# Attention of a hybrid encoder layer: the first product of the next pair but one begun within a pair's last two blocks, and a third gate of the sample made there

## The chip, the cores and the metric

The kernel runs on one core of one Trainium2 chip. The metric is the device time of one execution in microseconds. The median of the three runs of the kernel before is 2042.07 us (2040.25 to 2045.98).

The engines go by the names of the profile: PE is TensorE's matmul side and PEld its loading of weights, DVE is VectorE, ACT is ScalarE, POOL is GpSimd, SP is SyncE, which issues most DMAs. Each engine works through its own queue in order.

## The reference, cut to what matters

One encoder layer is applied to two groups of tokens, a prompt (1 x 1024 tokens) and a sample (1 x 512 tokens), each with 16 learned meta tokens in front. D_MODEL is 1024, there are 8 attention heads of 64, and the grid of tokens is 64 wide, so the prompt has 16 rows and the sample 8.

```
def encoder_layer(x, w_in, rel_bias, meta_bias, w_branch_na, w_branch_fn, w_out, g_mix, g_mlp, w_up, w_down):
    h = rmsnorm(x, g_mix)
    z = h @ w_in
    q, k, v, u, gate_na, gate_fn = jnp.split(z, ...)
    y_na = neighbourhood_attention(q, k, v, rel_bias, meta_bias) @ w_branch_na
    y_fn = fourier_mix(u) @ w_branch_fn
    mixed = sigmoid(gate_na) * y_na + sigmoid(gate_fn) * y_fn
    x = x + mixed @ w_out
    a = relu(rmsnorm(x, g_mlp) @ w_up)
    return x + (a * a) @ w_down
```

In neighbourhood_attention each grid token attends to 8 rows x 16 columns around it and to the 16 meta tokens. All is float32.

## The kernel before, in words

**Order of the whole.** The sample goes first, then the prompt. For each of the two, `run` (L328) reads and normalizes the tokens into hT (the normalized input, transposed, tokens along the free axis), projects the values, runs `attention` (L470), then `gates` (L720: the two gates of 1024 channels as 16 products with a sigmoid, 8 slices of 128 channels each), the merge of the attention branch, the Fourier branch, the output projection and the MLP.

**Precision.** A float32 product is made of three matmuls on operands that are split into a high and a low part: high x high, high x low, low x high. For a weight, ACT writes the high part (L151, or L154 with a scale) and another engine the low part (L152 on POOL or, where `lo_engine` says so, on DVE; L155 on DVE). `weights` (L141) loads a raw weight tile over SP's queue (L145) and splits it. The raw, high and low tiles have two buffers each, so a weight can be split only when the product before the last has ended.

**Attention.** Heads are handled in four pairs (`pr` 0 to 3). `project(pr)` (L493) is a generator that makes k and q of a pair: k in chunks of positions (two of 264 for the sample; 352, 344 and 344 for the prompt), q in chunks of 512 (one for the sample, two for the prompt). Each chunk is a `product` (L483) of eight steps of three matmuls (L487 to L489), and the generator yields after each step; after the eighth it evicts the chunk (L521 to L531 for k, L543 with L132 and L133 for q). At its very start it fetches and splits the weights of k and q (L495), takes the four tiles for q and k (L496, L497; four buffers per kind, that is two pairs' worth) and has POOL write the zero columns of k (L502).

`units(pr)` (L567) yields the pair's blocks: 8 for the sample and 16 for the prompt. A block (`unit`, L575) is itself a generator of three stages:

- scores: two matmuls (L594, L595), then bias and maximum on DVE (L599), the exponential on ACT (L601), reciprocal and scaling on DVE (L602, L603);
- transposes of the scores on PE into a PSUM tile `ps_t` of which there are two (L607), split by ACT (L132) and DVE (L133) into `pt`;
- the products with the values (L627), and after four blocks the eviction through `ot` (L632, one buffer) and `os` (L633), stored by L636.

`step` (L662) runs the first stage of a block together with the second stage of the block two before it and the third stage of the block four (sample) or three (prompt) before it. After each of the three it calls `between`.

**What is fed in between.** While a pair's blocks run, `feed` takes steps from a chain `nxt` (L672): the projections of the next pair, then steps of `early_gates` (L638), which makes some of the first gate's slices ahead of time: 24 matmuls a slice in the sample, evicted through `ot` (L646) and stored to DRAM (L647); `gates` loads them back (L728) and only applies the sigmoid (L735). `quota` (L657) says how many products of 512 positions of the gates are fed in each pair: none, none, none and 2 for the sample, 4, 2, 2 and 4 for the prompt. The number of steps, with four more that are empty, is spread evenly over the first slots of the pair; a block has three slots, and except in the last pair the two last blocks are left out of the count:

```
slots = 3 * (nu + lags[-1] if pr == 3 else nu - 2)
step(x, lambda s: feed(min(steps, (3 * u + s + 1) * steps // slots)))
```

With 28 steps (24 and the four empty ones) over 18 slots in the sample's pairs 0 to 2, the last real step falls into the sixth of eight blocks, and the two last blocks get none. Pair 3 has 16 real steps over 36 slots, the last 12 of which belong to the stages that run out.

**Gates.** `gates` runs over eight slices and makes, for each, first the attention gate (skipped where it was made early) and then the Fourier gate. Beside its products it runs generators from a list `beside` (L386 to L393), each with the count of the first product and the end: `fold_u` beside products 0 to 7 and `fold` (the folding of positions) beside products 6 to 13. There are 14 products in the sample.

**Order within a queue.** The framework plans each engine's queue from the program: an instruction comes as early as its inputs and its engine allow by the plan, and the earlier one in the program goes first where several could. `pinned` and `behind` (L110, L114) hold an instruction behind earlier ones. On the chip the queues then run in the planned order.

## Time and profile before

| what | value |
|---|---|
| median of three runs | 2042.07 us |
| lowest and highest run | 2040.25, 2045.98 us |
| profiled execution, its own time | 2044.82 us |
| span of its instructions | 2043.0 us |
| mean granted PE clock | 0.986 |
| sample's attention, first scores to last value product | 70.44 to about 162.0 us |
| prompt's attention, first scores to last value product | 824.27 to about 1049 us |

The profile's page gives, for each engine, the busy time, its share of the span and the number of instructions. The view of busy time by windows gives the same for stretches of time, with the clock that PE was granted: 1.00 is full speed. The view of waits says for which engine and line an engine's instructions waited. The timeline lists instructions in order of time, with the idle time of the engine ahead of one and what ended it in square brackets. The chain is the sequence of work that ended last, followed back from the end.

### The profile page before, as it was taken

The page shows a single profiled execution, that of the slowest core. Times are in us where ns is not written, and L with a number is a line of the kernel's source. Part 1 is how long each engine was busy: PE and PEld are TensorE (multiplying, and loading weights), DVE is VectorE, ACT ScalarE, POOL GpSimd, SP SyncE. Part 2 cuts the span into 40 slices and gives each one's busy share as a digit, 9 for nine tenths or more (in the row PEclk, how much of TensorE's full clock was granted, in tenths as well). Part 3 has the DMA queues.
Part 4 walks back from the last instruction along what each step waited for, and adds up shares of the span by engine and source line. Part 5 has one row for each costly group of instructions (what it writes and reads, how often), then busy time and mean ns, then how long its engine had stood idle before and what let it go on. Part 6 is the DMA issues. An engine that isn't in the chain of part 4 may idle for free.

```text
span 2043.0 us, 26403 instructions
## 1 busy us (share of the span) xinstructions
PE 1958.7 (96%) x9611; PEld 1626.4 (80%) x9611; DVE 1135.8 (56%) x1913; ACT 755.5 (37%) x1322; POOL 955.7 (47%) x744
## 2 busy tenths in 40 slices
PE   6989979999999999999999999999999999999997
PEld 4877867788888878888888888787788878888886
DVE  6572535667665553566663235567777677342246
ACT  3564413333333231455562313124333333533342
POOL 3224525366677641132243225203787785644442
PEclk9999989999999999999999999999999999999999
DMA  6655872345544445454555444322445444976663
GB/s 203 168 140 187 233 222 86 106 132 179 160 135 144 155 160 204 113 137 127 138 184 176 127 123 133 111 69 76 165 145 198 146 171 168 314 236 204 194 192 124
DMA packets 275363, 325.96 MB, mean 160 GB/s; under 512 B 42840, under 2 KB 197208, under 8 KB 274680
## 3 DMA queue, kind: packets, MB, share of 16 engines
q1 hardware_dynamic: 261504, 303.40, 46.7%
q0 software_dynamic: 13728, 20.88, 4.5%
q8 instruction: 75, 1.23, 0.3%
q14 instruction: 56, 0.46, 0.1%
HBM read 235.41 MB, written 91.37 MB: 160 GB/s over the span
## 4 chain that ended last, share of the span: by engine, by line
PE 82%; DVE 7%; DMA 3%; issue 2%; ACT 2%; POOL 2%; SPq 0%; ACTq 0%; DVEq 0%; POOLq 0%
PE ps_mm L128 22%; PE ps_o L128 20%; PE ps_s L128 18%; PE ps_t L128 7%; PE ps_mm L487 3%; PE ps_mm L488 3%; PE ps_mm L489 3%; PE ps_o L627 2%; PE ps_t L607 1%; DVE hn L873 1%; DVE gate L878 1%; POOL w_lo L152 1%; PE ps_s L594 1%; DVE gate L872 1%; DMA w_raw<-in_w_in 1%
## 5 line engine op out<-in xcount | busy, mean ns | idle before, releaser
L152 POOL TENSOR_TENSOR w_lo<-w_raw,w_hi 128x1024 fp32r<-128x1024 f32 x85 | 215.5, 2543 | 229.9 <-ACT w_hi L151 201.4
L151 ACT CAST w_hi<-w_raw 128x1024 fp32r<-128x1024 f32 x100 | 104.7, 1049 | 171.4 <-PE ps_s L128 48.9
L1056 DVE TENSOR_TENSOR relu<-relu 128x512 f32<-128x512 f32 (+1 forms) x34 | 66.7, 1960 | 108.2 <-ACT relu L1055 108.1
L487 PE MATMUL ps_mm<-hT,w_hi 128*128 128x512 f32 (+3 forms) x312 | 122.0, 391 | 0.0
L489 PE MATMUL ps_mm<-hT,w_lo 128*128 128x512 f32 (+3 forms) x312 | 113.0, 362 | 0.0
L488 PE MATMUL ps_mm<-hT,w_hi 128*128 128x512 f32 (+3 forms) x312 | 112.8, 361 | 0.0
L1293 POOL TENSOR_TENSOR x<-w_hi,x 128x512 fp32r<-128x512 f32 (+1 forms) x42 | 78.6, 1871 | 22.8 <-ACT x L1296 22.8
L601 ACT ACTIVATE sc<-sc,ast 128x288 f32<-128x288 f32 (+4 forms) x96 | 53.8, 561 | 83.8 <-DVE ast L599 83.0
L152 POOL TENSOR_TENSOR w_lo<-r,w_hi 128x1024 fp32r<-128x1024 f32 x15 | 35.9, 2395 | 95.3 <-ACT w_hi L151 95.3
L711 POOL MEMSET bm<- 64x96 f32 (+2 forms) x64 | 11.9, 185 | 143.2 <-DVE ast L599 98.8
L627 PEld LDWEIGHTS ps_o<-pt,vb 104*64 104x64 f32 (+6 forms) x576 | 62.5, 166 | 14.6 <-ACT pt L132 3.7
L627 PE MATMUL ps_o<-pt,vb 104*64 104x128 f32 (+6 forms) x576 | 65.5, 249 | 7.0 <-ACT pt L132 2.9
L152 POOL TENSOR_TENSOR w_lo<-w_hi 128x1024 fp32r<-128x1024 f32 x18 | 46.0, 2553 | 49.6 <-ACT w_hi L151 45.8
L128 PE MATMUL ps_t<-gate,x 128*128 128x512 f32 x264 | 65.5, 397 | 2.7 <-DVE r_lo L1404 2.7
L152 POOL TENSOR_TENSOR w_lo<-w_lo,w_hi 128x1024 fp32r<-128x1024 f32 x18 | 46.0, 2557 | 46.2 <-ACT w_hi L151 46.2
L489 PEld LDWEIGHTS ps_mm<-hT,w_lo 128*128 128x128 f32 x312 | 59.8, 192 | 8.0
L564 POOL TENSOR_TENSOR vb<-vr,vb 96x384 fp32r<-96x384 f32 (+4 forms) x48 | 48.4, 1023 | 37.8 <-ACT vb L563 37.7
L599 DVE CUSTOM_DVE_ANT_0 sc<-ps_s,bm 128x288 f32<-128x288 f32 (+4 forms) x96 | 46.3, 483 | 34.3 <-PE ps_s L595 18.2
L128 PE MATMUL ps_mm<-gate,x 128*128 128x512 f32 x256 | 64.2, 395 | 0.0
L487 PEld LDWEIGHTS ps_mm<-hT,w_hi 128*128 128x128 f32 x312 | 60.3, 193 | 2.3
L488 PEld LDWEIGHTS ps_mm<-hT,w_hi 128*128 128x128 f32 x312 | 60.4, 194 | 2.2
L128 PEld LDWEIGHTS ps_t<-gate,x 128*128 128x128 f32 x264 | 48.7, 188 | 16.1 <-DVE r_lo L1404 5.2
(670 smaller groups left out, 5885.3 us busy)
## 6 DMA issues: line engine op xcount, KB each, us to landing
w_raw<-in_w_in SPq DMA_DIRECT2D x56, 512.0 KB
w_raw<-in_w_up SPq DMA_DIRECT2D x34, 512.0 KB
wt<-hn SPq DMA_DIRECT2D x32, 512.0 KB
hidden_prompt<-h SPq DMA_DIRECT2D x32, 512.0 KB
w_hi<-hidden_prompt SPq DMA_DIRECT2D x20, 512.0 KB
w_raw<-hidden_prompt SPq DMA_DIRECT2D x18, 512.0 KB
w_lo<-hidden_prompt SPq DMA_DIRECT2D x18, 512.0 KB
w_raw<-in_w_out SPq DMA_DIRECT2D x16, 512.0 KB
```

Source lines behind the costliest of these rows:

```text
L128: self.nc.tensor.matmul(out, a, b, start=(i == 0 and not more), stop=(i == len(terms) - 1), skip_group_check=more)
L151: nc.scalar.copy(out=hi, in_=raw)
L152: (lo_engine or nc.gpsimd).tensor_tensor(out=lo, in0=raw, in1=hi.bitcast(F32), op=ALU.subtract)
L487: nc.tensor.matmul(ps, a[0], b[0], start=(kt == 0), stop=False)
L488: nc.tensor.matmul(ps, a[0], b[1], start=False, stop=False)
L489: nc.tensor.matmul(ps, a[1], b[0], start=False, stop=(kt == 7))
L564: nc.gpsimd.tensor_tensor(out=lo, in0=vs, in1=hi.bitcast(F32), op=ALU.subtract)
L599: nc.vector.tensor_tensor_reduce(out=sc[:, :W], in0=ps[:, :W], in1=bm[:, :W], scale=1.0, scalar=3e38, op0=ALU.add, op1=ALU.min, accum_out= ...
L601: nc.scalar.activation(out=sc[:, :W], in_=sc[:, :W], func=AF.Exp, bias=st[:, 0:1], scale=-1.0, accum_out=st[:, 1:2])
L627: nc.tensor.matmul(po[:m, j * 128:(j + 1) * 128], v, x, start=(i == 0), stop=(i == len(ops) - 1))
L1056: nc.vector.tensor_tensor(out=r, in0=r, in1=r, op=ALU.mult)
L1293: self.nc.gpsimd.tensor_tensor(out=to, in0=x, in1=y, op=op)
```

## The change

The change has three parts.

1. In `project`, the tiles for q and k and the zero columns on POOL are taken only after the eighth step of the first k product. The seven steps before need only the weights, hT and a PSUM bank.
2. The main loop of `attention` feeds steps in the two last blocks as well. The four empty steps go. All that is due in a pair is spread over the slots up to the two last blocks (in pair 3 over all slots); in the six slots of the two last blocks, seven steps of the *next but one* pair's projections are fed, 1, 1, 1, 1, 1 and 2. In pair 2, which has no next but one, the seven steps come from the early gates. The next pair then has seven steps fewer to do: 17 in the sample's pairs 1 and 2, 17 in its pair 3 (three gates, less seven); in the prompt 72, 49, 49 and 25.
3. The sample's last pair makes three early gates instead of two (`quota`), so that `gates` has 13 products instead of 14, and `fold` begins beside product 5 instead of 6.

The order of the products among themselves stays as it was.

```
-                          (fold, 6, 14)]
+                          (fold, 5, 13)]
...
         def project(pr):
             wk, wq = w0 if pr == 0 else self.qk_weights(pr)
-            qs = [p.tile([128, T], F32R, name="q", tag="q", bufs=4) for _ in range(2)]
-            ks = [p.tile([128, 2, nslot, 64], F32R, name="k", tag="k", bufs=4) for _ in range(2)]
-            state[pr] = (qs, ks)
             halves = slice(0, 64), slice(64, 128)
-            for k in ks:
-                for s in (0, nslot - 1):
-                    nc.gpsimd.tensor_copy(k[:, :, s, 16:64].rearrange("p i (g c) -> p i g c", g=2)[:, :, :, 0:8],
-                                          self.zero[:, None, None, 0:8].to_broadcast([128, 2, 2, 8]))
...
             for ci, (c0, cn) in enumerate(kch):
                 ps = self.psum("mm" if pr else None)
                 yield from product(ps[:, :cn], wk, slice(c0, c0 + cn))
+                if ci == 0:
+                    qs = [p.tile([128, T], F32R, name="q", tag="q", bufs=4) for _ in range(2)]
+                    ks = [p.tile([128, 2, nslot, 64], F32R, name="k", tag="k", bufs=4) for _ in range(2)]
+                    state[pr] = (qs, ks)
+                    for k in ks:
+                        for s in (0, nslot - 1):
+                            nc.gpsimd.tensor_copy(k[:, :, s, 16:64].rearrange("p i (g c) -> p i g c", g=2)[:, :, :, 0:8],
+                                                  self.zero[:, None, None, 0:8].to_broadcast([128, 2, 2, 8]))
...
-        quota = (0, 0, 0, 2) if T == 512 else (4, 2, 2, 4)
+        quota = (0, 0, 0, 3) if T == 512 else (4, 2, 2, 4)
...
+        begun = 7
+        filler = project(1)
+        left = 8 * (T // 512 + len(kch))
         for pr in range(4):
-            nxt = chain(project(pr + 1) if pr < 3 else (), islice(early, 8 * quota[pr]))
-            steps = 8 * (quota[pr] + (T // 512 + len(kch) if pr < 3 else 0)) + 4
+            due = left + 8 * quota[pr]
+            nxt = chain(filler, islice(early, 8 * quota[pr]))
+            if pr < 2:
+                filler, left = project(pr + 2), 8 * (T // 512 + len(kch)) - begun
+            else:
+                filler, left = islice(early, begun if pr == 2 else 0), -begun
             fed = 0
-            def feed(upto):
+            def feed(x, s):
                 nonlocal fed
+                main = 3 * (nu + lags[-1] if pr == 3 else nu - 2)
+                at = 3 * x + s + 1
+                upto = min(due, at * due // main) + max(0, (at - main) * begun // (3 * nu - main) if pr < 3 else 0)
                 while fed < upto:
                     fed += 1
-                    next(nxt, None)
-            slots = 3 * (nu + lags[-1] if pr == 3 else nu - 2)
+                    next(nxt if fed <= due else filler, None)
             for u, x in enumerate(chain(units(pr), [None] * lags[-1] if pr == 3 else ())):
-                step(x, lambda s: feed(min(steps, (3 * u + s + 1) * steps // slots)))
+                step(x, lambda s: feed(u, s))
             for _ in nxt:
                 pass
```

## The prediction

> **What bounds the kernel now.** I read the page first. TensorE (PE) is busy almost throughout, so a change that computes the same products can only win where PE idles or runs at a lower clock.

> ```profile
> PE 1958.7 (96%) x9611; PEld 1626.4 (80%) x9611; DVE 1135.8 (56%) x1913; ACT 755.5 (37%) x1322; POOL 955.7 (47%) x744
> ```

> The change touches the two attention stages. I cut the sample's (70 to 162 us) into stretches with the view of busy time by windows, each pair's last two blocks and the start of the next pair cut out (two of the eight full stretches between are left out here; the sum is over all). Columns: stretch, length, busy us (instructions) of PE, PEld, DVE, ACT, POOL, granted clock, DMA share, GB/s.

> ```profile
> 70.44:84.14 13.70, 12.61 (x80) 10.82 (x81) 8.67 (x30) 8.03 (x23) 4.55 (x11) 1.00 0.89 198
> 84.14:88.69 4.55, 1.64 (x15) 1.23 (x14) 4.46 (x10) 4.09 (x10) 2.53 (x3) 0.87 1.11 169
> 88.69:94.35 5.66, 5.66 (x29) 5.62 (x29) 4.67 (x17) 3.30 (x9) 1.45 (x6) 0.50 0.95 203
> 94.35:109.12 14.77, 14.77 (x110) 13.56 (x109) 9.72 (x30) 8.28 (x23) 4.22 (x11) 1.00 0.75 182
> 109.12:114.92 5.80, 2.90 (x26) 2.53 (x26) 5.31 (x14) 4.65 (x14) 2.47 (x6) 0.99 0.72 186
> 114.92:118.19 3.27, 3.27 (x17) 3.25 (x17) 2.45 (x9) 1.80 (x6) 0.25 (x1) 0.50 0.60 160
> 132.98:138.79 5.81, 2.51 (x23) 2.17 (x23) 5.33 (x14) 5.07 (x15) 2.25 (x5) 1.00 0.57 154
> 138.79:141.84 3.05, 3.05 (x13) 2.74 (x14) 2.76 (x9) 1.71 (x6) 1.36 (x2) 0.50 0.42 102
> 154.44:162.04 7.60, 6.96 (x51) 5.65 (x51) 5.01 (x15) 5.27 (x12) 3.44 (x5) 1.00 0.32 87
> sum 91.60, PE 80.75 PEld 72.30 DVE 65.85 ACT 58.43 POOL 30.60; mean PE 10.09 PEld 9.04 DVE 8.23 ACT 7.30 POOL 3.82
> ```

> Each of the three changes of pair has the same two parts: first PE idles (4.55-1.64 = 2.91, 2.90 and 3.30 us), then it runs saturated at clock 0.50 for 5.66, 3.27 and 3.05 us. In between (94.35 to 109.12) it is full at clock 1.00. Who PE waited for, by the view of waits for the sample and the timelines of PE and VectorE (DVE) at the second change:

> ```profile
> PE ps_t L607 <- DVE pt L133: 7.7, 5, 2.5
> PE ps_t L607 <- DVE sc L603: 2.6, 3, 1.2
> 112.64 0.53 PE L607 MATMUL ps_t<-ident,sc 128*96 128x128 f32 x3 [2.09 <-DVE pt L133]
> 114.92 0.85 PE L607 MATMUL ps_t<-ident,sc 128*96 128x128 f32 x3 [0.81 <-DVE sc L603]
> 109.48 1.23 DVE L155 SCALAR_TENSOR_TENSOR w_lo<-w_raw,w_hi 128x1024 fp32r<-128x1024 f32 x1 [0.99 <-ACT w_hi L154]
> 110.81 0.69 DVE L133 TENSOR_TENSOR q<-ps_mm,q 64x512 fp32r<-64x512 f32 x1
> 111.53 0.72 DVE L603 TENSOR_SCALAR sc<-sc,ast 128x288 f32<-128x288 f32 x1
> 112.17 0.41 DVE L133 TENSOR_TENSOR pt<-ps_t,pt 108x256 fp32r<-108x256 f32 x1
> ```

> When the projections run out, PE has only blocks, and they hang on DVE, which just then also splits the next pair's weights and evicts q. DVE is the local bound (busy 5.31 of 5.80 us), PE the bound elsewhere.

> The prompt shows the same, more mildly and without a drop of the clock:

> ```profile
> 883.79:890.00 6.21, 4.78 (x37) 4.04 (x37) 5.70 (x14) 5.22 (x13) 3.27 (x7) 1.00 0.61 177
> 939.51:950.00 10.49, 8.33 (x63) 7.48 (x63) 8.55 (x22) 7.01 (x18) 4.27 (x12) 1.00 0.58 156
> 995.99:1006.00 10.01, 7.77 (x55) 6.32 (x55) 8.73 (x24) 7.51 (x20) 3.96 (x10) 1.00 0.58 161
> 1006.00:1047.00 41.00, 40.72 (x280) 35.12 (x278) 27.12 (x77) 25.48 (x62) 14.67 (x30) 1.00 0.41 117
> 1047.00:1052.00 5.00, 4.09 (x20) 3.33 (x21) 2.44 (x4) 2.34 (x4) 3.08 (x2) 1.00 0.45 148
> ```

> Idle: 1.43, 2.16, 2.24, then 0.28 and 0.91 us in the last pair, which has less filler in its last blocks.

> **The change, part by part.** Products keep their order and number; seven of the eight steps of one are moved into each pair's last two blocks, where feeding has stopped. A step is three matmuls. Its price is the distance of two L487 rows: 0.37 us for the sample's k, 0.70 for q or a gate, 0.48 for the prompt's k.

> ```profile
> 94.64 0.29 PE L487 MATMUL ps_mm<-hT,w_hi 128*128 128x264 f32 x1
> 95.01 0.29 PE L487 MATMUL ps_mm<-hT,w_hi 128*128 128x264 f32 x1
> 103.28 0.40 PE L487 MATMUL ps_mm<-hT,w_hi 128*128 128x512 f32 x1
> 103.98 0.40 PE L487 MATMUL ps_mm<-hT,w_hi 128*128 128x512 f32 x1
> 824.54 0.32 PE L487 MATMUL ps_mm<-hT,w_hi 128*128 128x352 f32 x1
> 825.02 0.33 PE L487 MATMUL ps_mm<-hT,w_hi 128*128 128x352 f32 x1
> ```

> Sample: 7 x 0.37 = 2.6 us of filler at the first two changes of pair, 7 x 0.70 = 4.9 at the third (a gate). I take the smaller of two limits. By PE: the filler that fits into the idle time, plus half of the cold stretch (clock 0.50): 2.6+2.8 = 5.4; 2.6+1.6 = 4.2; 3.3+1.5 = 4.8. By DVE: the stretch cannot get shorter than DVE's work in it, so what DVE idles there plus the filler: (10.21-9.13)+2.6 = 3.7; (9.07-7.76)+2.6 = 3.9; (8.86-8.09)+4.9 = 5.7. Smaller ones: 3.7+3.9+4.8 = 12.4 us. The last pair is fed up to its last slot, which covers the 0.64 us idle at the end (7.60-6.96).

> Prompt: 3.4 us (k) or 4.9 (gate) of filler against 1.43, 2.16 and 2.24 of idle, no cold clock: up to 5.8; the last pair's 0.28+0.91 = 1.2 on top.

> Together 12.4+0.6+5.8+1.2 = 20.0 us if nothing new is waited for. I charge back 3: the other stretches get thinner filler (17 steps where there were 24, so 14.77-2.6 = 12.2 us with DVE's 9.72 in it, 80% instead of 66%). Bounds: nothing (at 66% PE never idled), or the boundary's own rate, 2.9 us idle at 86 to 91%, once more for each of three pairs, 8.7; I take 0.5 for each of six, since 80% lies between and each block has two blocks' distance between its stages.

> The third early gate takes 24 matmuls out of the gates stage and puts eight steps into attention: -5.55 and +8 x 0.70 = 5.6, so 0. The chain shows one such product, all PE:

> ```profile
> 222.03 5.55 PE ps_o L128 x24
> 173.61 0.46 PE L244 MATMUL ps_mm<-relu,w_hi 128*128 128x128 f32 x2 [1.42 <-DMA w_hi<-in_w_uT]
> 215.31 0.46 PE L244 MATMUL ps_mm<-relu,w_hi 128*128 128x128 f32 x2 [0.48 <-DVE w_lo L133]
> ```

> Its low half (1.23 us) goes from POOL to DVE, which has room in the last pair. One more store and load stand in SP's queue ahead of the u weights, for which PE waits 1.42 us: between -1.42 and +1.42, I take 0, because the eviction that precedes them is no longer held by a gate's store. The fold beginning one product earlier overlaps the other fold in three products instead of two; the overlap cost 0.48 at 215.31, so +0.5 at most. The k tiles' zero columns on POOL come after a product instead of before it: they are due only at the next pair's scores, a whole pair later; 0.

> What is moved in front of others: the weights' loads in SP's queue and their splits on ACT and DVE get an earlier place in the program. The wait added: PE, in order, now meets the new product's low half (L489) within the last two blocks; behind it stand those blocks' transposes and value products. The splits in the trace that it needs:

> ```profile
> 81.06 1.23 DVE L152 TENSOR_TENSOR w_lo<-w_raw,w_hi 128x1024 fp32r<-128x1024 f32 x1 [2.11 <-ACT w_hi L151]
> 103.22 1.23 DVE L152 TENSOR_TENSOR w_lo<-w_raw,w_hi 128x1024 fp32r<-128x1024 f32 x1 [0.20 <-ACT w_hi L151]
> 127.08 1.23 DVE L152 TENSOR_TENSOR w_lo<-w_raw,w_hi 128x1024 fp32r<-128x1024 f32 x1 [0.26 <-ACT w_hi L151]
> 869.59 1.23 DVE L152 TENSOR_TENSOR w_lo<-w_raw,w_hi 128x1024 fp32r<-128x1024 f32 x1 [0.32 <-ACT w_hi L151]
> ```

> They are done at 82.3, 104.5, 128.3 and 870.8; the last two blocks begin at 84.1, 109.1, 133.0 and, in the prompt, one block ahead of 883.8. Cover 1.8 us at the first change, over 4 at the others: no cost; without cover each us of lateness is one of PE.

> The clock term rests on the rows: idle gaps of 2.09 and 0.81 us are followed by 0.50, while the first stretch, with 1.09 us idle in all, stayed at 1.00. [...]

> Sum: -17. The profiled execution took 2044.82 us (span 2043.0), so 2027.8; it lay 2.75 above the median of 2042.07, so the median becomes 2025.

> **Rivals.** (1) DVE sets the pace of the whole sample stage. For: at the changes it is 86 to 91% busy. Against: PE ran full beside it. If the chain score, exponential, scaling, transposes cannot keep DVE busier than three quarters, its 65.9+1.2 us of work (all stretches together, and the third gate) take 89.4 us, against 91.6+5.6 of before with the gate: -7.8, with the prompt's -4 2030. (2) The clock stays down. If something other than the gaps brings it to 0.50 there, filling them leaves it so. What the clock adds to my sum is 1.1+1.3+1.5 = 3.9 us (the three smaller limits beyond the filler), so -13 and 2029. For: nothing but the sequence. Against: the full stretches at 1.00 have the same instructions without the gaps. [...] (3) The change does not do what it says: the framework plans the order of PE's queue itself, and where it takes the weights for late it puts the new steps behind the last blocks; 2042. Against: L487 follows program order in the timeline. (4) Slower: the begun product blocks PE. From a weight split 1.8 us (first change) or over 4 us (others) later than now, each of the six changes loses all further lateness, with the blocks behind it. A raw weight load that is issued only when it is needed takes 5.6 us, and the low split 1.2:

> ```profile
> 297.15 5.64 DMA w_raw<-in_w_out
> 304.17 1.03 PE L128 MATMUL ps_o<-w_hi,us 128*128 128x266 f32 x2 [9.68 <-ACT us L132]
> ```

> That is 6.9 us at six places, in place of idle times of 2.5 us on average (2.91, 2.90, 3.30, 1.43, 2.16, 2.24): 6 x 4.4 = 26, less the 1.8 us won at the ends of the two stages, 2066. It decides from stalls of 2.8 us at each change. Against it stands the cover above. The second row is the largest stall near by (a load placed ahead of an eviction in ACT's queue); if the shifted start of things moves it, up to 9.7 us go either way, which I only let into the range.

> **How the numbers follow.** My forecast 0.55; DVE's pace 0.2; clock 0.1; no effect 0.08; slower 0.05; 0.02 for more gain than I see. A measurement of this kernel can tell about 0.3% (6 us) from no change. Faster 0.87, same 0.08, slower 0.05. The forecast alone reaches from 2022 (nothing charged back) to 2028. For 8 in 10 the upper end takes in rivals 1 and 2 and half of their gain lost again, 2036; the lower end adds half of the ACT stall, 2017.

> **What would show it.** In the changed profile the two granted 0.50 stretches and the idle before L607 at the changes of pair are gone or below 1 us; L487 rows stand between the L594 rows of the last two blocks; the sample's attention stage, from its first L594 to its last L627, takes about 84 us (91.6-13+5.6) and the prompt's some 5 us less; the gates stage has one x24 product fewer. I am wrong if PE waits there for w_lo, if equal idle time turns up in the middle of pairs, or if the clock stays at 0.50 without long gaps.

## The result, and the profile after

The changed kernel takes 2032.38 us in the median of six runs (2030.07 to 2037.26), the kernel before 2042.55 in six: a ratio of 0.9950, 95% interval 0.9934 to 0.9967, or 7 to 13 us less. Measured once more later, the ratio was 0.9931 (0.9917 to 0.9945), 11 to 17 us less. I forecast 17; the profiled execution, 2034.05 us with a span of 2032.3, shows 10.7 (2043.0 before). One execution of the dummy filler's kernel below, 3263.92 us at a mean granted clock of 0.558, is left out of its ratio.

PE does the same 9611 instructions and is busy 3.4 us less than the 1958.7 of before:

```profile
PE 1955.3 (96%) x9611; PEld 1622.2 (80%) x9611; DVE 1138.2 (56%) x1914; ACT 756.4 (37%) x1323; POOL 961.9 (47%) x743
```

The three changes of pair of the sample, in the view of busy time by windows (columns as in the prediction), each from the scores of its last two blocks into the next pair; then the whole of the prompt's attention:

```profile
85.06:91.70 6.64, 6.24 (x56) 6.09 (x55) 5.72 (x16) 5.26 (x13) 3.94 (x8) 1.00 0.98 184
105.56:112.26 6.70, 6.29 (x56) 6.14 (x55) 5.78 (x17) 5.26 (x13) 3.88 (x7) 1.00 0.90 234
126.14:134.48 8.34, 8.34 (x53) 7.19 (x52) 6.70 (x20) 6.38 (x16) 3.55 (x5) 1.00 0.89 212
817.54:1038.20 220.66, 216.69 (x1401) 191.59 (x1400) 143.24 (x383) 128.80 (x301) 66.56 (x167) 1.00 0.51 130
```

Idle time at the three changes is 0.40, 0.41 and 0 us where it was 2.91, 2.90 and 3.30, and the granted clock is 1.00 in all four windows: both parts of the old pattern are gone. The timeline of PE shows why; between the scores (L596) of pair 0's last blocks now stand steps of pair 2's first product, up to the next pair's first scores:

```profile
87.16 0.26 PE L596 MATMUL ps_s<-k,q 128*128 128x216 f32 x1
87.37 0.30 PE L487 MATMUL ps_mm<-hT,w_hi 128*128 128x264 f32 x1
87.75 0.49 PE L609 MATMUL ps_t<-ident,sc 128*96 128x128 f32 x3
87.99 0.37 PE L487 MATMUL ps_mm<-hT,w_hi 128*128 128x264 f32 x1
89.51 0.26 PE L596 MATMUL ps_s<-k,q 128*128 128x216 f32 x1
```

What PE waits for now, by the view of waits, in the sample's attention and in its gates stage (us in total, times, longest):

```profile
PE ps_t L609 <- DVE sc L605: 3.0, 6, 0.8
PE ps_t L609 <- DVE pt L133: 2.4, 2, 1.5
...
PE ps_mm L244 <- DVE w_lo L133: 2.7, 1, 2.7
PE ps_s L128 <- POOL w_lo L152: 2.2, 1, 2.2
```

The first two lines were 2.6 and 7.7 us before; of what is left, 3.9 us lie in the first and the last pair. The last two are new: the gates stage, where PE waited 1.42 and 0.48 us before, loses 4.9. The longest wait of the last pair, 1.54 us before a transpose at 153.87, leads to a scaling on DVE that took 1.88 us where another run of it below takes 0.32, and stood beside a POOL instruction that ended with it:

```profile
151.47 1.88 DVE L605 TENSOR_SCALAR sc<-sc,ast 128x216 f32<-128x216 f32 x1
153.28 0.54 DVE L133 TENSOR_TENSOR pt<-ps_t,pt 96x384 fp32r<-96x384 f32 x1
...
206.89 2.64 DVE L835 TENSOR_TENSOR gain<-hT,hT 128x264 f32<-128x264 f32 x1
209.71 0.42 DVE L837 TENSOR_TENSOR acc<-gain,acc 128x263 f32<-128x263 f32 x1
```

```profile
150.85 2.37 POOL L152 TENSOR_TENSOR w_lo<-w_raw,w_hi 128x1024 fp32r<-128x1024 f32 x1 [0.42 <-ACT w_hi L151]
...
206.58 2.66 POOL L152 TENSOR_TENSOR w_lo<-w_raw,w_hi 128x1024 fp32r<-128x1024 f32 x1 [4.61 <-ACT w_hi L151]
```

POOL's two end at 153.22 and 209.24, DVE's at 153.35 and 209.53; DVE's next instructions are short again. This is the suspicion that several experiments below try.

By stage, from the timeline of PE of every profile (the gates' first part runs from their first product to the end of the long wait for `us` ahead of the Fourier branch, 304.17 in the trace of before, so it includes that wait):

| kernel | sample attention | of it pairs 2 to 4 | gates, first part | prompt attention | ratio to before |
|---|---|---|---|---|---|
| before | 91.60 | 72.15 | 142.1 | 224.4 | 1 |
| changed | 88.33 | 68.77 | 140.6 | 220.7 | 0.9950 |
| changed, again | 89.36 | 69.24 | 139.7 | 221.8 | 0.9931 |
| two gates | 85.17 | 66.60 | 143.2 | 221.6 | 0.9939 |
| third gate only | 96.49 | 76.48 | 142.0 | 224.8 | 1.0019 |
| dummy filler | 91.28 | 71.10 | 142.1 | 228.7 | 1.0011 |
| begun four | 90.18 | 70.51 | 140.7 | 222.2 | 0.9976 |
| three low halves on DVE | 89.14 | 68.04 | 137.7 | 221.3 | 0.9938 |
| foldings apart | 87.37 | 68.75 | 136.5 | 222.0 | 0.9920 |
| both of these | 86.28 | 65.94 | 136.6 | 223.5 | 0.9921 |
| all low halves on DVE | 86.32 | 67.57 | 135.1 | 221.9 | 0.9905 |
| the same, foldings apart | 86.53 | 67.66 | 135.4 | 221.3 | 0.9912 |
| the same, last change of prompt with three steps | 87.25 | 67.10 | 135.2 | 220.3 | 0.9917 |
| prompt's values on DVE | 87.42 | 68.84 | 140.6 | 219.3 | 0.9941 |

Read small differences with care: the first pair of the sample alone took 18.6 to 21.1 us among kernels that are alike there. The first blocks wait for the tables of biases, whose loads come sooner or later from one execution to the next; the maximum of the second block, in the changed kernel and in the one with the foldings apart:

```profile
73.34 0.46 DVE L601 CUSTOM_DVE_ANT_0 sc<-ps_s,bm 128x288 f32<-128x288 f32 x1 [0.66 <-DMA bm<-g_un]
```

```profile
71.54 0.46 DVE L601 CUSTOM_DVE_ANT_0 sc<-ps_s,bm 128x288 f32<-128x288 f32 x1 [0.39 <-PE ps_s L597]
```

That is why the table has pairs 2 to 4 by themselves. The prompt's attention, too, lies between 220.7 and 223.5 in the eight profiles with the changed code there. All eight have the same two waits of PE in the last pair, 0.5 and 1.1 us. In five of them the clock falls to 0.50 for 3.4 us behind these (221.6 to 223.5 us); in three it stays at 1.00 (220.7 to 221.3).

### The profile page after: what moved, and what is told of

It is laid out like the page before. It is cut to its first block, busy times and chain, and to the rows that moved or that the text cites. A ratio compares the mean times of both kernels' runs of the same rounds, so it can differ in the third digit from the quotient of the medians.

```text
span 2032.3 us, 26413 instructions
## 1 busy us (share of the span) xinstructions
PE 1955.3 (96%) x9611; PEld 1622.2 (80%) x9611; DVE 1138.2 (56%) x1914; ACT 756.4 (37%) x1323; POOL 961.9 (47%) x743
## 4 chain that ended last, share of the span: by engine, by line
PE 77%; DVE 7%; DMA 5%; issue 4%; POOL 4%; ACT 3%; SPq 0%; POOLq 0%; DVEq 0%; ACTq 0%
PE ps_mm L128 22%; PE ps_o L128 20%; PE ps_s L128 17%; PE ps_t L128 7%; PE ps_mm L487 2%; PE ps_mm L488 2%; PE ps_mm L489 2%; PE ps_o L629 1%; POOL w_lo L152 1%; DVE hn L885 1%; PE ps_t L609 1%; DVE gate L890 1%; DMA w_raw<-in_w_in 1%; DMA gain<-in_w_fnB 1%; DMA w_raw<-in_w_out 1%
## 5 line engine op out<-in xcount | busy, mean ns | idle before, releaser
L152 POOL TENSOR_TENSOR w_lo<-w_raw,w_hi 128x1024 fp32r<-128x1024 f32 x84 | 212.4, 2537 | 228.1 <-ACT w_hi L151 202.8
L151 ACT CAST w_hi<-w_raw 128x1024 fp32r<-128x1024 f32 x100 | 104.8, 1049 | 168.5 <-PE ps_mm L128 49.9
L487 PE MATMUL ps_mm<-hT,w_hi 128*128 128x512 f32 (+3 forms) x320 | 125.9, 393 | 0.0
L488 PE MATMUL ps_mm<-hT,w_hi 128*128 128x512 f32 (+3 forms) x320 | 114.8, 359 | 0.0
L489 PE MATMUL ps_mm<-hT,w_lo 128*128 128x512 f32 (+3 forms) x320 | 114.7, 358 | 0.0
L603 ACT ACTIVATE sc<-sc,ast 128x288 f32<-128x288 f32 (+4 forms) x96 | 53.9, 562 | 78.4 <-DVE ast L601 78.0
L152 POOL TENSOR_TENSOR w_lo<-r,w_hi 128x1024 fp32r<-128x1024 f32 x15 | 35.9, 2395 | 96.7 <-ACT w_hi L151 96.7
L152 POOL TENSOR_TENSOR w_lo<-w_hi 128x1024 fp32r<-128x1024 f32 x18 | 47.1, 2615 | 48.7 <-ACT w_hi L151 48.7
L128 PE MATMUL ps_t<-gate,x 128*128 128x512 f32 x264 | 65.5, 397 | 2.7 <-DVE r_lo L1416 2.7
L152 POOL TENSOR_TENSOR w_lo<-w_lo,w_hi 128x1024 fp32r<-128x1024 f32 x18 | 45.9, 2551 | 45.6 <-ACT w_hi L151 45.6
L489 PEld LDWEIGHTS ps_mm<-hT,w_lo 128*128 128x128 f32 x320 | 60.1, 188 | 8.5
L128 PE MATMUL ps_mm<-gate,x 128*128 128x512 f32 x256 | 64.2, 395 | 0.0
L487 PEld LDWEIGHTS ps_mm<-hT,w_hi 128*128 128x128 f32 x320 | 60.6, 189 | 1.7
L128 PEld LDWEIGHTS ps_t<-gate,x 128*128 128x128 f32 x264 | 48.7, 188 | 16.1 <-DVE r_lo L1416 5.1
L601 DVE CUSTOM_DVE_ANT_0 sc<-ps_s,bm 128x288 f32<-128x288 f32 (+4 forms) x96 | 46.3, 482 | 26.9 <-PE ps_s L597 10.9
```

The source lines that it names most:

```text
L128: self.nc.tensor.matmul(out, a, b, start=(i == 0 and not more), stop=(i == len(terms) - 1), skip_group_check=more)
L151: nc.scalar.copy(out=hi, in_=raw)
L152: (lo_engine or nc.gpsimd).tensor_tensor(out=lo, in0=raw, in1=hi.bitcast(F32), op=ALU.subtract)
L487: nc.tensor.matmul(ps, a[0], b[0], start=(kt == 0), stop=False)
L488: nc.tensor.matmul(ps, a[0], b[1], start=False, stop=False)
L489: nc.tensor.matmul(ps, a[1], b[0], start=False, stop=(kt == 7))
```

## The experiments

The ratios are to the kernel before, run on the same chip; there are three groups of four runs, with medians of before of 2044.04, 2045.73 and 2043.00 us.

### Only two early gates

```diff
-        quota = (0, 0, 0, 3) if T == 512 else (4, 2, 2, 4)
+        quota = (0, 0, 0, 2) if T == 512 else (4, 2, 2, 4)
-                          (fold, 5, 13)]
+                          (fold, 6, 14)]
```

> The changed kernel with the third early gate taken back (the sample's last quota 2 instead of 3, the second folding from product 6 to 14 as before). Theory: the filler at the changes of pair brings the whole gain, and the third gate costs 2 to 5 us: 2.4 us of waits for DVE in the sample's last pair (where a POOL subtraction of a gate's low half stretches DVE's scaling), and 2.6 us in the gates stage. Without it the gates stage takes 5.55 less the 2.6 recovered = about 3 us more, the attention stage 5.6 + 2.4 less = 8 us less: 2027 to 2029. The last pair then has 9 steps of filler instead of 17 over 36 slots; thinner filler may leave some tenths of a us idle, so up to 2030. Rival: the third gate is what fills the last pair; without it PE idles there as long as the gate took (5.6 us), the attention stage stays at 88.3 us and the gates stage gets its product back: 2035 to 2038.

Measured: 2030.41 us, 0.9939 (0.9927 to 0.9952), no different from the changed kernel. So the begun products alone bring the whole gain. But the theory's sum came out by luck: the attention got 3.2 us shorter, not 8, for 5.6 us of work taken out, and the gates 2.5 longer (first part). The view by windows shows what happened in the last pair, where 9 steps of filler are spread over 36 slots:

```profile
134.00:135.00 1.00, 0.48 (x3) 0.15 (x2) 1.00 (x3) 0.89 (x2) 0.20 (x1) 1.00 0.25 89
135.00:136.00 1.00, 1.00 (x10) 0.86 (x9) 1.00 (x4) 0.28 (x1) 0.21 (x1) 1.00 0.31 72
136.00:137.00 1.00, 0.28 (x2) 0.07 (x2) 0.80 (x4) 1.00 (x3) 0.00 (x0) 1.00 1.00 292
137.00:138.00 1.00, 1.00 (x5) 0.86 (x6) 0.30 (x3) 0.96 (x4) 0.71 (x2) 0.77 1.05 323
138.00:139.00 1.00, 1.00 (x8) 0.90 (x6) 0.96 (x2) 1.00 (x4) 1.00 (x1) 0.50 0.39 121
```

There are two waits for DVE, of 0.52 and 0.72 us, and the clock falls to 0.50 until 144. The rival had half a point: the third gate is also filler for the last pair. Net, it is a wash in the changed kernel, within the 2 to 3 us that the intervals leave.

### Only the third gate

```diff
-        quota = (0, 0, 0, 2) if T == 512 else (4, 2, 2, 4)
+        quota = (0, 0, 0, 3) if T == 512 else (4, 2, 2, 4)
-                          (fold, 6, 14)]
+                          (fold, 5, 13)]
```

This is the kernel before with those lines.

> The kernel before with only the third early gate added (quota 3, the second folding one product earlier); the changes of pair stay as they were. Theory: the gate's work is a wash (5.6 us in, 5.55 out) and its side costs come alone: about 2.6 us in the gates stage (PE waits for POOL's low half where it waited 1.42 us for the u weights, and 2.7 us where the two foldings overlap in three products) and some of the 2.4 us in the last pair; 2044 to 2047. The three stretches at clock 0.50 are still there. Rival 1: the gate is free, 2042.5, and the missing microseconds of the changed kernel come from the begun products. Rival 2: the gate fills idle of the last pair (0.64 us) and nothing else, 2042.

Measured: 1.0019 (1.0009 to 1.0029), 2 to 6 us slower, as the theory had it; both rivals fall. The attention grew by 4.9 us (5.6 less the idle of 0.64 at its end), and the gates' first part, which should have lost 5.55, stayed at 142.0. The waits of PE there are others than the theory named, though:

```profile
PE ps_o L128 <- ACT w_hi L151: 2.8, 1, 2.8
PE ps_s L128 <- ACT w_hi L151: 1.7, 1, 1.7
PE ps_mm L244 <- DVE w_lo L133: 1.2, 1, 1.2
```

Behind the wait of 2.8 us the clock is 0.50 from 183.4 to 186.8, which by my estimate, half of these 3.4 us, costs up to 1.7 us more.

### A filler that is thrown away

```diff
+        def dummy():
+            ps = self.psum("mm")[:, :kch[0][1]]
+            for kt in range(7):
+                e = hT[0][:, kt, 0:128]
+                for i in range(3):
+                    nc.tensor.matmul(ps, e, hT[i % 2][:, kt, 0:kch[0][1]], start=(kt == 0 and i == 0), stop=(kt == 6 and i == 2))
+                yield
```

It is fed in the last two blocks of the kernel before, in the first three pairs.

> The kernel before, whose three first pairs get seven steps of three matmuls in their last two blocks that belong to no product: their result is thrown away, the outputs stay the reference's, and no work is moved from the rest of the pair. A step is as long as one of k's (0.37 us in the sample, 0.48 in the prompt): 2.6 us a change in the sample, 3.4 in the prompt. This tells the clock from the idle time. Theory: the 2 us gaps bring the clock down; with them filled it stays at 1.00, the cold stretches of 5.66, 3.27 and 3.05 us shrink to half (-2.8, -1.6, -1.5), and the filler goes into 2.9, 2.9 and 3.3 us of idle time: the sample's attention takes about 86 us instead of 91.6. In the prompt, 3.4 us of filler meet 1.4, 2.2 and 2.2 of idle: +4 at most. In all 2037 to 2042. Rival: something else than the gaps (the loads, the splits of weights, the change of pair itself) brings the clock down; it is 0.50 after each change although PE has work, the sample's attention stays at 91 us or grows by up to 3, and the kernel takes 2043 to 2050.

Measured: 2047.22 us, 1.0011 (1.0002 to 1.0020), above the theory's 2037 to 2042 by 5, of which the slower kernel before in that group makes 1.5. By stage it says what it was made for. The windows around the three changes:

```profile
84.00:88.00 4.00, 2.56 (x22) 2.14 (x20) 3.91 (x9) 3.83 (x9) 1.97 (x2) 1.00 1.09 181
88.00:94.00 6.00, 5.71 (x50) 5.71 (x51) 4.50 (x15) 2.92 (x9) 1.88 (x6) 1.00 0.85 183
112.00:116.00 4.00, 4.00 (x37) 4.00 (x37) 3.02 (x11) 1.81 (x5) 0.96 (x5) 1.00 0.79 177
135.00:140.00 5.00, 2.77 (x18) 2.08 (x17) 1.77 (x7) 2.44 (x6) 1.46 (x2) 1.00 0.53 134
140.00:145.00 5.00, 4.85 (x25) 4.12 (x26) 3.85 (x15) 2.73 (x10) 1.14 (x3) 0.66 0.62 175
```

At the first two changes the clock stays at 1.00 with the same loads, splits and change of pair as before; what is different is that PE has work. At the third the idle time moved on into the last pair, as one wait of 2.33 us that ends at 140.09, and 1.6 us behind it the clock falls. So the gaps bring the clock down, and the rival falls. The sample's attention took 91.28 us with 7.8 us more work than before, 8.1 less than the sum; PE's idle time fell from 10.85 to 7.04, so 3.8 of it is idle time filled and about 4.3 the clock. The theory's 86 us was wrong because it counted this work as free: the filler fitted the idle time at the changes, but idle time that remained, 2.33 us, came up later. In the prompt 10.1 us of filler cost 4.3, as the theory allowed.

### The first three low halves on DVE

```diff
-                w = self.weights(self.rows("w_in", c0 + dm * 128))
+                w = self.weights(self.rows("w_in", c0 + dm * 128), lo_engine=nc.vector if T == 512 and done < 3 else None)
```

> The changed kernel with one thing moved: in the sample's gates stage the low halves of the first three weights are written by DVE (1.23 us each) instead of POOL (2.4 us each). Theory: POOL's subtractions hold DVE's instructions until they end (the scaling of 128x216 took 1.88 us instead of 0.33 beside one of 2.37 us), and in the gates stage the third product waits for its low half because POOL's queue has a subtraction ahead of it that hangs on the last pair's values. With DVE in POOL's place the wait of 1.54 us in the last pair and that of 2.24 us at the beginning of the gates stage go, and DVE has room there: -3 to -4, so 2028 to 2030. Rival: the waits end with something else (ACT's high half, the weight's load, DVE's own queue): DVE's low halves come just as late or hold up the last pair's transposes themselves, and the time is the same, 2031 to 2034.

Measured: 2030.34 us, 0.9938 (0.9925 to 0.9952): in the theory's 2028 to 2030 or just off it, but not to be told from the changed kernel by the total. Where it acts, it acts as forecast. The same scaling and the wait of PE behind it:

```profile
152.58 1.23 DVE L152 TENSOR_TENSOR w_lo<-w_raw,w_hi 128x1024 fp32r<-128x1024 f32 x1 [0.97 <-ACT w_hi L151]
...
154.25 0.32 DVE L605 TENSOR_SCALAR sc<-sc,ast 128x216 f32<-128x216 f32 x1
```

```profile
154.72 0.40 PE L609 MATMUL ps_t<-ident,sc 128*108 128x128 f32 x2 [0.61 <-DVE sc L605]
```

The scaling takes 0.32 us instead of 1.88, the wait is 0.61 instead of 1.54, pairs 2 to 4 take 68.0 instead of 68.8 or 69.2. In the gates the wait for POOL's low half (2.24) is gone; their first part takes 137.7 us instead of 140.6 or 139.7.

### The foldings apart

```diff
-                          (fold, 5, 13)]
+                          (fold, 8, 13), (fold, 8, 11)]
```

> The changed kernel with the second folding moved out of the first one's way: it runs beside products 8 to 12 of the gates, twice a product beside 8 to 10, instead of once beside each of 5 to 12, so that it no longer overlaps the folding of u (products 0 to 7). Theory: the 2.73 us that PE waits at 215 us for u's low half are the price of that overlap (VectorE's queue has both foldings in turn, and one of its instructions is stretched to 2.64 us there); the wait goes and the time falls by 2 to 3 us against the changed kernel on the same chip. Rival: the wait belongs to the place of u's products in PE's queue, or two steps of the folding a product make VectorE late somewhere else; no change within 1 us.

Measured: 2028.69 us, 0.9920 (0.9906 to 0.9933), against 0.9931 (0.9917 to 0.9945) of the changed kernel beside it: 2.2 us in the theory's sense, which the totals don't prove. The waits of PE in the gates do show the step:

```profile
PE ps_s L128 <- POOL w_lo L152: 2.1, 1, 2.1
PE ps_o L128 <- ACT w_hi L151: 0.2, 1, 0.2
```

The 2.7 us behind u's low half are gone, the wait for POOL stays, and the first part of the gates takes 136.5 us: the third gate's 5.55 are back in full (142.1 less 5.55 is 136.6).

### Both repairs

Both edits of the two sections above.

> Both repairs of the third gate's side costs at once: the first three low halves of the sample's gates on DVE, and the second folding beside products 8 to 12. Theory: the two costs (2.24 and 1.54 us by POOL's subtractions, 2.73 us by the overlap of the foldings) are independent and add up; -5 us against the changed kernel on the same chip. Rival: they are the same cost seen twice (PE's queue in the gates stage only gives the time back at the next wait); -2.5 us as with the low halves alone.

Measured: 2030.09 us, 0.9921 (0.9909 to 0.9934). They don't add up in the total, as the rival had it: the gates' first part is 136.6 us as with the foldings alone. PE does wait less there (0.8 us for the u weights, where it waited 2.1 for POOL). What gives the time back is the end of the stage. From the eviction of `uc`, the last that PE's products release, to that of `us`, which ends the long wait, the view of the chain runs over loads, DVE and ACT, not over PE. Its two ends, with the foldings alone and with both repairs:

```profile
264.39 0.39 ACT uc L132
292.73 0.27 ACT us L132
```

```profile
262.81 0.39 ACT uc L132
292.37 0.27 ACT us L132
```

Counted from the stage's start (156.49 and 156.11), PE comes to `uc` after 107.9 and 106.7 us, 1.2 us sooner with both. But the chain behind it is 1.2 us longer, mainly since three loads of `gain` in it take 14.5 us in all instead of 13.0, and the wait for `us` grows from 9.68 to 11.32 us. So the rival's reason, one cost seen twice, is not what the trace shows.

### All low halves of the sample's gates on DVE

```diff
-                w = self.weights(self.rows("w_in", c0 + dm * 128))
+                w = self.weights(self.rows("w_in", c0 + dm * 128), lo_engine=nc.vector if T == 512 else None)
```

> The changed kernel with the low halves of all the sample's gates, 13 of them, written by DVE instead of POOL. Theory: each POOL subtraction of 2.4 us holds one DVE instruction for its whole length, also in the foldings (2.44, 2.64 and 2.59 us where the like take 0.42); with none left, the stretched instructions go and DVE, which is busy 27 of 78 us in this stage, takes the 16 us more of work easily. The wait of 2.73 at 215 us goes too, since the stretched instruction at 206.9 was in its way; -4 to -6 us against the changed kernel on the same chip. Rival: the low halves now stand in DVE's queue behind the folding and come late to PE; the waits for w_lo grow, and it is no faster than the kernel with three of them moved, -2.5 or worse.

Measured: 2025.84 us, 0.9905 (0.9891 to 0.9918), the fastest of all, about 5 us below the changed kernel beside it (0.9931). None of the folding's instructions of L835 to L838 is stretched any longer (2.44, 2.64 and 2.59 us in the changed kernel). Two later ones, at 240.7 and 243.1, still take 1.09 and 1.51 us instead of 0.42, beside POOL's 1.30 and 1.32 us for other operands. Of the waits of PE in the gates up to 232 us only short ones are left:

```profile
PE ps_mm L244 <- DMA w_hi<-in_w_uT: 1.0, 1, 1.0
PE ps_o L128 <- ACT w_hi L151: 0.2, 1, 0.2
```

The low halves come in time although DVE has 16 us more to do. The foldings still overlap here; so the 2.73 us were not the price of the overlap as such, but of the overlap with one instruction in it held for 2.2 us.

### The changed kernel again

> The changed kernel once more, unaltered, so that the other runs of this group can be set against it on the same chip; 0.995 of the kernel before, within 0.002.

Measured: 2031.86 us, 0.9931 (0.9917 to 0.9945), 0.002 below the 0.995 that was expected, at the edge of it. In its profile PE waits at the same places as in the first one, but the clock falls behind three of them: behind the 1.54 us of the sample's last pair, which ends at 153.45, behind 2.19 us in the gates (215.8 to 219.2), and behind the two waits of the prompt's last pair. The sample's and the prompt's stretch:

```profile
151.91:154.36 2.45, 0.91 (x10) 0.91 (x10) 2.45 (x4) 0.70 (x2) 0.89 (x1) 1.00 0.21 33
154.36:157.77 3.41, 3.41 (x13) 2.83 (x13) 0.52 (x2) 0.89 (x2) 1.27 (x1) 0.50 0.32 92
1017.93:1021.34 3.41, 3.41 (x17) 3.00 (x15) 2.28 (x8) 1.49 (x5) 0.37 (x3) 0.50 0.49 135
```

The sample's last pair takes 26.9 us here and 25.4 in the first profile.

### Four steps instead of seven

```diff
-        begun = 7
+        begun = 4
```

> The changed kernel with four steps of the begun product in each pair's last two blocks instead of seven: 1.5 us of filler at the sample's first two changes instead of 2.6, 2.8 instead of 4.9 at the third; 1.9 and 2.8 in the prompt instead of 3.4 and 4.9. Theory: the gain at a change is the filler up to the idle time, and the clock stays up as long as no idle of 2 us is gathered in a few us; with 1.5 us of filler against 2.9 of idle, 1.4 us per change stay, the clock holds, and what comes back in the last pairs (3.0 us idle in the sample's, 1.6 in the prompt's) partly goes. Sample attention 88 to 90 us against 88.3 and 89.4 of the two profiles with seven, prompt 220 to 222 against 220.7 and 221.8: the same total within 2 us. Rival: the clock needs the whole filler; it falls to 0.50 at a change again and the sample's attention takes 91 us or more, +2 to +4 in all.

Measured: 2038.66 us, 0.9976 (0.9967 to 0.9986), some 5 to 9 us slower than with seven steps, so the theory's "same total" is wrong. Its clock is right at the changes: 1.00 at all three. The 2 us of idle that it names for the clock were my estimate; no run shows such a limit. The three fewer steps a change showed up as 1.3 to 1.7 us in pairs 2 to 4. The prompt is within its scatter. One drop of the clock in the sample's attention came in the first pair, behind a single wait of 1.43 us:

```profile
74.00:76.00 2.00, 0.89 (x7) 0.67 (x6) 1.07 (x5) 1.13 (x5) 0.51 (x3) 1.00 0.76 179
76.00:77.00 1.00, 0.69 (x5) 0.69 (x6) 0.91 (x4) 0.98 (x3) 0.23 (x1) 0.88 0.88 237
77.00:78.00 1.00, 1.00 (x7) 1.00 (x6) 1.00 (x5) 0.47 (x2) 1.00 (x2) 0.50 1.17 262
```

The profile, with a span of 2035.6 one of the shorter executions, has 0.8 to 1.9 us more than the changed kernel's in the sample's attention; where the rest is lost stays open.

### All low halves on DVE, and the foldings apart

> The kernel with all low halves of the sample's gates on DVE (0.9905 of the kernel before), and the second folding moved clear of the first as well. Theory: both repairs remove the same wait at 215 us (PE for u's low half, late because DVE was held by POOL in the middle of two foldings), so the second adds nothing: 0.9905 within 0.0015. Rival: the overlap costs DVE's time beside the holding; 1 to 2 us more.

Measured: 2026.13 us, 0.9912 (0.9899 to 0.9926): the second repair adds nothing once POOL no longer holds DVE in the foldings' overlap. The theory holds.

### The prompt's values on DVE

```diff
-                nc.gpsimd.tensor_tensor(out=lo, in0=vs, in1=hi.bitcast(F32), op=ALU.subtract)
+                (nc.vector if T == 1024 else nc.gpsimd).tensor_tensor(out=lo, in0=vs, in1=hi.bitcast(F32), op=ALU.subtract)
```

> The changed kernel with the low halves of the values in the prompt's attention written by DVE instead of POOL (1.0 to 1.1 us each on POOL, some 0.5 us on DVE to judge by the evictions of pt of the same width). Theory: of the prompt's 4.0 us of idle time 2.3 are waits for POOL's low half of the values, the first of each pair; these go, the rest stays: the prompt's attention takes 218 to 219.5 us against 220.7 and 221.8, 1 to 2 us less in all. Rival: DVE, 65% busy there, is what the blocks hang on; 16 more of such pairs in its queue, ahead of the scaling and the evictions, bring as many waits for DVE as they take away; no change, or up to 3 us more.

Measured: 2030.87 us, 0.9941 (0.9928 to 0.9953); the total can't show 1 us. The prompt's attention took 219.3 us, below all eight profiles with POOL there (220.7 to 223.5). Waits of PE in it, of the changed kernel and of this one:

```profile
PE ps_o L629 <- POOL vb L566: 2.3, 6, 0.5
PE ps_o L629 <- DVE pt L133: 1.1, 1, 1.1
PE ps_o L629 <- ACT pt L132: 0.5, 1, 0.5
```

```profile
PE ps_o L629 <- DVE vb L566: 1.4, 5, 0.5
PE ps_o L629 <- DVE pt L133: 0.8, 3, 0.3
```

The theory's stage time came out, but the wait for the values became shorter rather than going: 2.3 to 1.4 us.

### Three steps at the prompt's last change

```diff
-                filler, left = islice(early, begun if pr == 2 else 0), -begun
+                last = begun if T == 512 else 3
+                filler, left = islice(early, last if pr == 2 else 0), -last
```

This is on top of all low halves on DVE.

> The kernel with all low halves of the sample's gates on DVE, and in the prompt's third change three steps of the gate instead of seven (2.1 us of filler, against 2.24 us of idle before). Theory: the seven steps were more than the change could use, and the four that return to the last pair fill the idle time that came up there (0.5 and 1.1 us at about 20 us into it, 0.4 and 0.2 by values); the prompt's attention takes 1 to 1.5 us less. Rival: the idle time in the last pair does not come from thinner filler but from that place itself (DVE's queue there); it stays, and the change of pair gets a wait back: no change or 0.5 us more.

Measured: 2026.62 us, 0.9917 (0.9903 to 0.9931), beside 0.9905 and 0.9912 without it. By profile the prompt's attention took 220.3 us instead of 221.3 and 221.9, and the waits of 0.5 and 1.1 us in the last pair are gone. So they came from thinner filler, and the clock stays at 1.00 there, but the totals show no gain.

## Why the prediction was right, and where it was not

**Right: the mechanism.** Idle gaps at the changes of pair, closed by moved steps; the 0.50 stretches gone; no wait for the new product's low half there. Rival 2 (the clock stays down) falls by the profile and by the dummy filler, rival 3 (no effect) by the timeline, and rival 4 (the begun product blocks PE) by the idle 0.40, 0.41 and 0 us at the changes. Rival 1 (DVE's pace) had 2030, closer than my 2025, and 89.4 us for the sample's attention, which took 88.3 and 89.4. But that is luck: its condition, DVE never busier than three quarters, does not hold. In pairs 2 and 3 of the changed kernel DVE is busy 17.1 of 20.5 and 18.9 of 22.9 us, 83%, with PE at 96%; the average of 75% comes from the first and the last pair. The clock was worth 3.9 us in my sum; the dummy filler gives about 4.3, and the changed kernel 4.6 (8.9 us gained in the sample's attention, 4.2 of them idle time of PE). In the experiments the clock fell to 0.50 behind 2.33 us (dummy filler), behind 1.43 (begun four), and behind 0.52 and 0.72 within 3 us (two gates). But a gap of 2 us does not always cost the clock, as my clock term took it: behind 2.24 and 2.73 us in the gates of the changed kernel it stayed at 1.00.

**The sample's changes: -12.4, -0.6, +1.5 charged.** That is -11.5; measured were -8.9 (91.60 to 88.33 with 5.6 us more work), and -7.8 in the second profile. At the changes 8.3 us of idle time went, but 4.1 came back elsewhere. The step that failed is the charge: thinner filler was priced at 0.5 a pair from DVE's share of the time, evenly. Most of it fell on the last pair instead, which has 17 steps over 36 slots: PE's waits there are 0.65, 0.85 and 1.54 us, 3.0 in all, against 0.64 before. About 0.9 of the 1.54 us was POOL holding DVE, shown by the low halves on DVE (0.61 left). The rest is filler in part: with 24 steps in that pair (third gate only) PE has no such wait, although a scaling is held there too (1.43 us at 161.39). But the kernel before spaced its 16 steps and four empty ones as the kernel with four begun steps spaces its 20, and that one has 2.3 us of waits there, not 0.64; what else makes the difference stays open. The second profile's last pair is about 1.5 us longer than the first's, with the clock at 0.50 behind the 1.54. The first pair, where the late tables show, took 18.6 to 21.1 us among kernels alike there.

**The third gate: -5.55 and +5.6.** The second half held, since its steps are PE work in a stage where PE is full. The first failed: the gates' first part fell by 1.5 and 2.4 us only. I had the wait for the u weights (-1.42 to +1.42) and the overlap of the foldings (at most 0.5); the overlap cost 2.2 us more (2.73 against 0.48), and a wait that I had not on the list, 2.24 us for POOL's low half, took the place of the 1.42. Nor had I priced DVE being held beside POOL: in the trace its 0.32 became 1.88 beside POOL's 2.37 us and its 0.42 became 2.64 beside 2.66, and both are gone with the low halves on DVE. I priced POOL's work as if it lay beside DVE's, though the trace of before has such rows too: a scaling of 1.40 us at 153.35, beside POOL's 2.39 from 152.19, and a folding of 2.63 us at 209.31, beside 2.65 from 209.01. With the third gate and without POOL's subtractions that stage's first part is 7.0 us shorter than before (142.1 to 135.1), more than the 5.55.

**The prompt: -5.8, -1.2, +1.5 charged.** That is -5.5; measured were -3.8 and -2.6. I let the moved steps fill all idle time at the changes. Idle time in that attention fell from 6.7 to 4.0 us: each pair's first values still wait for POOL's low half (0.48, 0.47, 0.53), which filler does not shorten, and 1.6 us of waits came up in the last pair, whose steps had been moved away; three steps instead of seven removed those. In the second profile they also cost a stretch at 0.50.

**Sum.** -17 forecast; the same terms as the profile shows them are -8.9, -3.8 and, for the gate, +4.1 in its first part (-1.5 instead of -5.55); the start, the stretch behind the Fourier wait and the rest moved by -0.5, -1.5 and -0.2, which is also the size of the scatter: -10.7 in all, with the roundings. The large wait of 9.68 us for `us` hardly moved (9.30; 9.2 to 11.3 in all profiles), so the range was wider below than it had to be.

## What to carry to other kernels

Fill a gap where queues run dry with steps of work that is due anyway, and look where those steps are missing afterwards: here most of the time lost again lies in the last pair, which has the fewest. Before counting work on two engines as parallel, look in the timeline for instructions that take several times their usual length (1.88 us for 0.32 here), and see what ends with them: here moving POOL's 13 subtractions to the busier DVE was worth another 5 us (0.9905 against 0.9931 of the kernel before). A gap counted about double here (4.2 us less idle time in the sample's attention brought 8.9 us, with the 0.50 stretches gone), so price it with the slow stretch that may follow, and look at more than one execution: behind the same 1.54 us the clock fell in one profile and not in the other. And before adding up what two repairs save in a stage, see whether the stage's end hangs on the engine that they relieve.

## What the runs showed of the hardware

In the changed kernel's trace two DVE instructions on SBUF alone were held until a POOL tensor_tensor ended: 1.88 us instead of 0.32 and 2.64 instead of 0.42, each beside one on POOL of 2.4 to 2.7 us that ended 0.13 and 0.29 us before it. Of the 42 such that began beside a POOL tensor_tensor in the first 310 us, 19 took over 0.1 us longer than their shortest run. Those with an operand in PSUM were not held: of the 35 that began so in the same time, none took over 0.03 us longer; three evictions (L133) of 0.42, 0.16 and 0.42 us stand beside the 2.41 us on POOL at 189.47.
